# Five more seven-product quads in the SSM branch product, left factors fetched for each use, and side transfers moved to the queues of ScalarE and GpSimd

## The chip, the cores and the metric

The kernel runs on one core of one Trainium2 chip. Its engines are TensorE (PE, matrix products; PEld is its weight load), VectorE (DVE), ScalarE (ACT), GpSimd (POOL) and SyncE (SP, which here only issues transfers). SP, ACT and POOL can each start DMA transfers, each from a queue of its own that is worked off in order. The metric is the device time of one execution in microseconds.

## The reference

One layer of a hybrid block on 256 tokens of width 2048, all in float32:

```
proj = rms_norm(x, norm_w) @ w_in                 # 2048 x 18496 (q, k, v, z_a, z_s, xbc, dt, g_a, g_s)
o_a  = dilated_attention(q, k, v) * silu(z_a)     # 16 heads of 128, three patterns
xbc  = silu(causal_conv(xbc)); xs, B, C = split(xbc)
y    = rms_norm((ssd_scan(xs, dt, a, B, C) + d_skip * xs) * silu(z_s), ssm_norm_w)     # 256 x 4096
merged = sigmoid(g_a) * (o_a @ w_attn_branch) + sigmoid(g_s) * (y @ w_ssm_branch)
out  = rms_norm(x + merged @ w_out, final_norm_w)
```

The product that the change works on is `y @ w_ssm_branch`: 256 x 4096 by 4096 x 2048.

## The kernel before

**Precision.** Every operand is split in two float32r parts, high `h` (a copy by ScalarE, line 276) and low `l` (what is left, a subtraction by VectorE, line 277). A product is the sum of three matmuls: high by high, high by low, low by high.

**The stream of weights.** All weights lie in DRAM in units of 128 x 1024 (512 KB), in the order of use. A unit is loaded by SP into one of five ring buffers (tag `w`, line 265), split by ScalarE and VectorE into `h` and `l` (four buffers each), and used by TensorE. `FIRST[tag]` is the number of the first unit of a product. A step of another part can be hung behind a unit: `behind_unit(n, f)` runs `f` when unit `n` has been split.

**Order of stages.** First product and dt; then eight groups of the SSM (tags B, C, xs, zs; two units of weights for each 128 columns), each with convolution, decays and scan; then the product `ssm` in two column pairs, `("ssm", 0)` and `("ssm", 2)`; then `v`, the 16 heads (q, k, za), and `ga`, `attn`, `out`, each in two column pairs. The scheduler of the language puts the instructions of each engine in an order of its own, by priorities; the semaphores follow from the buffers.

**Pair products.** `gemm_pair` computes 256 rows by two blocks of 512 columns, step by step over quads: a quad is 256 of the inner dimension. `S_QUADS` says which quads are done by seven products instead of eight (a Strassen-like scheme), `Y_ORDERS` in which order the quads of `ssm` come.
- A plain quad: two units, each split by one ACTIVATE and one subtraction of 128 x 1024, and 2 x 2 x 2 x 3 = 24 matmuls of 128 x 512.
- A seven-product quad: 7 x 3 = 21 matmuls of 128 x 512. Its right factors: `wa` (512 KB), a presummed `wt` (512 KB) and `wc` (256 KB) are loaded; ScalarE and VectorE split `wa`, `wc` and `wt`, VectorE subtracts (line 557) and splits the rest. If the sums were not made before (`presum`), the raw unit is loaded as `wb` and VectorE makes the two sums in place (lines 549 and 555).
- Its left factors: four sums of quarters of the activations, made by `turn_x` on VectorE, split, and kept as a tile `sx`.

**Side work in the group stage.** `sum_jobs` makes presums ahead: `get` loads two tiles (512 and 256 KB) into a `place`, `add` makes two subtractions of 128 x 512 three units later (`SUM_LAG`), and `spill` writes the result to DRAM. There is one place for the SSM's 18 slots (three per group, `SUM_UNITS`); 22 jobs stand in the list, so the last four of `("v", 2)` are not made ahead. `keep_left` makes left factors and spills them; `fetch_left` loads them again. Six of the eight left factors of `ssm` go this way; those of quads 12 and 13 are made in place by `left_y`. A left factor that serves both pairs is loaded once and stays in SBUF with three of its four parts, the fourth in the activations themselves (`spare`).

**Queues and pacing.** All of these transfers, the fetches and the spills, are issued by SP, between the loads of the stream. So that they do not start too early, GpSimd first copies one column of the unit's `h` into the first column of the destination (lines 247, 251, 432, 638, 903): the transfer has to wait for that copy. Only `x` and the last norm's weights near the end are issued by ScalarE's queue.

Of the kernel before, what the change touches and what calls it, by code (L numbers as in the profile page):

```python
# [9 lines left out]
F32 = mybir.dt.float32  # L10
F32R = mybir.dt.float32r
AF = mybir.ActivationFunctionType
# [3 lines left out]
P = 128  # L16
# [180 lines left out]
def hybrid_block(ctx: ExitStack, tc: tile.TileContext, wall, xt, x, pk_d, cst_d, fw_d, out):  # L197
# [32 lines left out]
    ssm_pool = []  # L230

    def behind_unit(n, f):
        on_unit.setdefault(n, []).append(f)
# [4 lines left out]
    def spill(kept, key, name, src, shape):  # L238
        kept[key] = dram.tile([P, *shape], F32, name=name, tag=name)
        nc.sync.dma_start(kept[key], src)  # L240

    def sum_jobs(jobs, units, places):

        def get(tag, q, t, b11, behind):
            n = FIRST[tag] + 2 * q
            for dst, src in ((t, wall[n + 1]), (b11, wall[n, :, :512])):
                gp.tensor_copy(dst[:, 0:1], behind)
                nc.sync.dma_start(dst, src)

        def add(tag, q, t, b11, res, behind):  # L250
            gp.tensor_copy(res[:, 0:1], behind)
            ve.tensor_tensor(res[:, :512], t[:, :512], b11, ALU.subtract)
            ve.tensor_tensor(res[:, 512:], t[:, 512:], res[:, :512], ALU.subtract)
            spill(presum, (tag, q), f"t_{tag[0]}{tag[1]}_{q}", res, [UNIT])

        for n, ((tag, q), u) in enumerate(zip(jobs, units)):
            t, b11, res = places[n % len(places)]
            behind_unit(u, lambda behind, a=(tag, q, t, b11): get(*a, behind))
            behind_unit(u + SUM_LAG, lambda behind, a=(tag, q, t, b11, res): add(*a, behind))

# [6 lines left out]
    def unit(n, shape):  # L267
        if n not in loaded:
            load(n)
        w = loaded.pop(n)  # L270
        h = stream.tile([P, UNIT], F32R, name=f"h{n}", tag="h", bufs=H_BUFS)
        l = stream.tile([P, UNIT], F32R, name=f"l{n}", tag="l", bufs=H_BUFS)
        cuts = (0, UNIT // 2, UNIT) if n < N_FINE else (0, UNIT)
        with tc.high_priority(L_AHEAD) if n >= KT // UB else nullcontext():
            for a, b in zip(cuts, cuts[1:]):
                ac.activation(h[:, a:b], w[:, a:b], AF.Copy)  # L276
                ve.tensor_tensor(l[:, a:b], w[:, a:b], h[:, a:b].bitcast(F32), ALU.subtract)  # L277
# [407 lines left out]
    with tc.tile_pool(name="ssm", bufs=2) as sp:  # L685
# [205 lines left out]
        for c in GS_BEFORE[0]:  # L891
            gates(("gs", c), th_s, yT, hr_x)

        sums_at = big.tile([P, 4, UNIT], F32, name="sums_at", tag="yo1b")
        at = sums_at[:, 3]
        begin = FIRST[("xs", 4)]
        sum_jobs(
            SUMS_SSM, [FIRST[("B", g)] + n for g in range(1, 7) for n in SUM_UNITS],
            [(sums_at[:, 0], sums_at[:, 2, :512], sums_at[:, 1])],
        )  # L900

        def left_x(q, behind):
            gp.tensor_copy(at[:, 0:1], behind)
            keep_left(("x", q), two_kts(XT, q), 0, at)

# [71 lines left out]
    with tc.tile_pool(name="xp", bufs=1) as xp:  # L977
        sxs = {}
        ssm_room = room_of(xp.tile([P, ROOM_SSM * 512], F32, name="room_s", tag="room"), 0, ROOM_SSM)

        def left_y(q):
            spare = Y_SPARE[q]
            sx = new_sx(xp, sum(s == spare for s in Y_SPARE.values()), spare, f"y{q}")
            sxs[q] = turn_x(sx, ring(f"sxt_y{q}").rearrange("p (n m) -> p n m", n=2), two_kts(yT, q), spare)

        for q in SX_Y:
            if q in Y_LATE:
                continue
            fetch_left(sxs, xp, sum(s == Y_SPARE[q] for s in Y_SPARE.values()), ("y", q), two_kts(yT, q), Y_SPARE[q], plain_unit(("ssm", 0), Y_ORDERS[0].index(q) - 3 if q in S_QUADS[("ssm", 0)] else 12, Y_ORDERS[0]))
        for c in (0, 2):  # L990
            es, prods = gemm_pair(
                ("ssm", c), lambda kt: kt_of(yT, kt), 2 * KT, sxs, c == 2, {} if c else {2: [scale_gate], **{u: [lambda q=q: left_y(q)] for q, u in Y_LATE.items()}},
                1, Y_ORDERS[c], ssm_room,
# [19 lines left out]
    dist_c, count_c = dc[:, :384], dc[:, 384:]  # L1013
    behind_unit(FIRST[("v", 2)] + 1, lambda behind: fetch(dc, cst_d[:, :768], behind))
    room = room_of(big.tile([P, 6 * 512], F32, name="room_v", tag="yo0a"), 2, 2)
# [17 lines left out]
    with tc.tile_pool(name="att", bufs=2) as ap:  # L1033
# [33 lines left out]
        def mix(h, pT, za):  # L1067
# [10 lines left out]
            if h % 2 == 1 and q in ATT_QUADS:  # L1078
# [3 lines left out]
            SUMS_ATT, range(FIRST[("q", 0)] + 7, N_UNITS, ATT_EVERY),  # L1082
            [
                (th_a[:, i, :UNIT], th_a[:, 1, UNIT + 512 * i : UNIT + 512 * i + 512], th_a[:, 0, UNIT:])
                for i in range(2)
            ],
        )
# [28 lines left out]
    with tc.tile_pool(name="fin", bufs=2) as fp:  # L1116
# [36 lines left out]
        for n in range(4):  # L1153
            i, cs = n // 2, slice(n % 2 * UNIT, (n % 2 + 1) * UNIT)
            behind_unit(
                FIRST[X_BEHIND[n][0]] + X_BEHIND[n][1],
                lambda behind, i=i, cs=cs: fetch(fin[:, i, cs], x[i * P : (i + 1) * P, cs], behind, nc.scalar),
            )

        fw = big.tile([P, D], F32, name="fw", tag="yo0b")  # L1160
        for n, (tag, u) in enumerate(FW_BEHIND):
            cs = slice(n * UNIT, (n + 1) * UNIT)
            behind_unit(
                FIRST[tag] + u, lambda behind, cs=cs: fetch(fw[:, cs], fw_d[cs].partition_broadcast(P), behind, nc.scalar)
            )
# [106 lines left out]
```

## Time and profile before

| | |
|---|---|
| median of 3 runs | 1385.53 us (1385.44 to 1386.13) |
| profiled execution, first to last instruction (span) | 1383.8 us |
| TensorE busy | 1373.6 us, 99% of the span |
| VectorE busy | 1169.5 us, 85% |
| ScalarE busy | 835.5 us, 60% |
| GpSimd busy | 142.0 us, 10% |
| DMA | 345.00 MB, mean 249 GB/s |
| granted TensorE clock | 0.998 |

The profile shows one execution. Its own time is known as its span; what lies around the span (the launch and the end) is not in it, and the median of the runs shown is 1.7 us longer than the span. A busy TensorE is not TensorE at its best: matmuls overlap, so the time from the start of one to the start of the next is what counts, not the duration of one.

### The profile page before, as it was taken

To read this page: it belongs to the slowest core of one execution; us is meant where nothing else is said; L and a number is where in the kernel's file an instruction comes from. 1 tells how busy PE (TensorE), PEld (TensorE's weight loads), DVE (VectorE), ACT (ScalarE), POOL (GpSimd) and SP (SyncE) were. 2 spreads that over 40 slices of the span, in tenths; PEclk is the share of its full clock that TensorE was granted. 3 is DMA by queue.
4 is the path that set the end of the run, shared out by engine and by line. 5 is a ranking of instruction groups with operands and counts; after the bars stand their busy time and mean duration, and the time that the engine had idled before them with its cause. 6 is when DMAs were issued, how large, how long until landed. Compare 5 with 4: busy or idle time off the path is not lost.

```text
span 1383.8 us, 20696 instructions
## 1 busy us (share of the span) xinstructions
PE 1373.6 (99%) x7266; PEld 1169.9 (85%) x7266; DVE 1169.5 (85%) x1753; ACT 835.5 (60%) x1306; POOL 142.0 (10%) x226
## 2 busy tenths in 40 slices
PE   9999999999999999999999999999999999999997
PEld 8888888888888888888888888888888888888886
DVE  7898999987799898789889897777877788888897
ACT  7656677675667675766565554544544556655564
POOL 2301111101011100010001001111111000000112
PEclk9999999999999999999999999999999999999999
DMA  9767988868787866668677668888888757865773
GB/s 347 231 187 225 313 254 291 279 224 287 245 266 240 294 212 208 188 224 280 230 259 267 222 209 278 275 275 273 299 288 301 241 161 264 294 222 180 243 273 122
DMA packets 105080, 345.00 MB, mean 249 GB/s; under 512 B 11728, under 2 KB 13712, under 8 KB 104976
## 3 DMA queue, kind: packets, MB, share of 16 engines
q1 hardware_dynamic: 103536, 339.62, 74.0%
q10 hardware_dynamic: 1440, 4.06, 0.8%
q8 instruction: 57, 0.93, 0.3%
q14 instruction: 47, 0.39, 0.1%
HBM read 314.87 MB, written 28.77 MB: 248 GB/s over the span
## 4 chain that ended last, share of the span: by engine, by line
PE 97%; DMA 1%; DVE 1%; ACT 1%; issue 0%; SPq 0%; POOL 0%; POOLq 0%; DVEq 0%; ACTq 0%
PE ps_zs L329 8%; PE ps_xs L329 8%; PE ps_zs L332 4%; PE ps_q L329 4%; PE ps_za L329 4%; PE ps_k L329 4%; PE ps_xs L332 4%; PE ps_ssm L476 3%; PE ps_ssm L477 3%; PE ps_ssm L478 3%; PE ps_q L332 2%; PE ps_k L332 2%; PE ps_za L332 2%; PE ps_gs L414 2%; PE ps_gs L412 2%; PE ps_gs L413 2%
## 5 line engine op out<-in xcount | busy, mean ns | idle before, releaser
L276 ACT ACTIVATE h<-w 128x1024 fp32r<-128x1024 f32 (+1 forms) x398 | 413.9, 1047 | 318.0 <-issue 78.8
L277 DVE TENSOR_TENSOR l<-w,h 128x1024 fp32r<-128x1024 f32 (+1 forms) x398 | 479.4, 1211 | 124.2 <-ACT h L276 121.8
L329 PE MATMUL ps_zs<-XT,h 128*128 128x512 f32 x496 | 176.3, 397 | 0.0
L329 PE MATMUL ps_xs<-XT,h 128*128 128x512 f32 x496 | 175.9, 396 | 0.0
L332 PE MATMUL ps_zs<-XT,l 128*128 128x256 f32 x496 | 139.9, 282 | 0.0
L332 PE MATMUL ps_xs<-XT,l 128*128 128x256 f32 x496 | 139.8, 282 | 0.0
L329 PEld LDWEIGHTS ps_xs<-XT,h 128*128 128x128 f32 x496 | 93.3, 188 | 21.7
L329 PEld LDWEIGHTS ps_zs<-XT,h 128*128 128x128 f32 x496 | 93.4, 188 | 21.2
L332 PEld LDWEIGHTS ps_zs<-XT,l 128*128 128x128 f32 x496 | 93.7, 189 | 1.5 <-issue 0.7
L332 PEld LDWEIGHTS ps_xs<-XT,l 128*128 128x128 f32 x496 | 93.7, 189 | 0.4
L329 PE MATMUL ps_q<-XT,h 128*128 128x512 f32 x256 | 92.5, 405 | 0.2 <-ACT h L276 0.2
L329 PE MATMUL ps_k<-XT,h 128*128 128x512 f32 x256 | 89.9, 395 | 0.0
L329 PE MATMUL ps_za<-XT,h 128*128 128x512 f32 x256 | 89.7, 394 | 0.0
L543 ACT ACTIVATE ha<-wa 128x1024 fp32r<-128x1024 f32 x43 | 45.4, 1055 | 46.4 <-DMA wa<-in_wall 10.9
L332 PE MATMUL ps_q<-XT,l 128*128 128x256 f32 x256 | 71.2, 278 | 0.0
L332 PE MATMUL ps_k<-XT,l 128*128 128x256 f32 x256 | 71.1, 278 | 0.0
L332 PE MATMUL ps_za<-XT,l 128*128 128x256 f32 x256 | 71.1, 278 | 0.0
L544 DVE TENSOR_TENSOR la<-wa,ha 128x1024 fp32r<-128x1024 f32 x43 | 52.5, 1220 | 11.9 <-ACT ha L543 11.8
L782 ACT ACTIVATE gt<-acb,acT 128x128 f32<-128x128 f32 x128 | 44.2, 391 | 23.7 <-DMA acb<-acum_d 21.9
L329 PEld LDWEIGHTS ps_q<-XT,h 128*128 128x128 f32 x256 | 48.2, 188 | 11.5 <-ACT h L276 0.6
L329 PEld LDWEIGHTS ps_za<-XT,h 128*128 128x128 f32 x256 | 48.1, 188 | 11.3
L329 PEld LDWEIGHTS ps_k<-XT,h 128*128 128x128 f32 x256 | 48.1, 188 | 11.2
(688 smaller groups left out, 3325.1 us busy)
## 6 DMA issues: line engine op xcount, KB each, us to landing
w<-in_wall SPq DMA_DIRECT2D x394, 512.0 KB, 4.7
wa<-in_wall SPq DMA_DIRECT2D x43, 512.0 KB, 4.9
th_a<-in_wall SPq DMA_DIRECT2D x19, 512.0 KB, 5.6
sums_at<-in_wall SPq DMA_DIRECT2D x18, 512.0 KB, 4.7
acb<-acum_d SPq DMA_DIRECT2D x32, 256.0 KB, 4.0
t_ssm<-sums_at SPq DMA_DIRECT2D x13, 512.0 KB, 4.1
wt<-t_ssm SPq DMA_DIRECT2D x13, 512.0 KB, 5.4
th_a<-in_wall SPq DMA_DIRECT2D x19, 256.0 KB, 6.0
```

The costliest lines, as they stand in the source:

```text
L276: ac.activation(h[:, a:b], w[:, a:b], AF.Copy)
L277: ve.tensor_tensor(l[:, a:b], w[:, a:b], h[:, a:b].bitcast(F32), ALU.subtract)
L329: pe.matmul(acc, h[:, kk, :], m, start=(kt == 0), stop=False)
L332: pe.matmul(acc[:, S:], l[:, kk, :], m[:, :S], start=False, stop=(kt == KT - 1))
L412: pe.matmul(accs[i], xh, h[:, kk], start=(kt == 0), stop=False)
L413: pe.matmul(accs[i], xh, l[:, kk], start=False, stop=False)
L476: pe.matmul(acc, xh, h, start=start, stop=False)
L477: pe.matmul(acc, xh, l, start=False, stop=False)
L478: pe.matmul(acc, xl, h, start=False, stop=stop)
L543: ac.activation(h, src, AF.Copy)
L544: ve.tensor_tensor(l, src, h.bitcast(F32), ALU.subtract)
L782: ac.activation(g4[:, n, b], acb[:, j, b // 2 * P : b // 2 * P + P], AF.Relu, scale=-1.0, bias=sc[:, h : h + 1],)
```

## The change

1. The lists of quads: `("ssm", 0)` has nine seven-product quads (5 to 13), not seven; `("ssm", 2)` has eleven (2, 3, 5 to 13), not eight. The orders of the quads are new, with up to four seven-product quads in a row. The left factors of quads 12 and 13 are made earlier (behind quads 3 and 4 of the first pair).
2. The left factors of the other nine quads are made with all four parts, spilled, and fetched anew for each use, into a ring of five buffers (`Y_RING`), three quads ahead (`Y_AHEAD`): 16 fetches of 512 KB, not five of 384 KB and one of 512 KB.
3. Presums for the SSM and v: five slots per group, not three; 27 jobs, all of them made, not 18. Two places, not one; the result overwrites the loaded tile.
4. The side fetches (`side`) are issued by ScalarE's queue, in its program order behind the `h` copy of the unit on which they hang (`issue_after`: a place in the order, no semaphore). The spills are issued by GpSimd's queue. The pacing copies on GpSimd are gone; the subtractions of `add` and the left factors of x stand behind the unit's `l` in VectorE's order.

```diff
 S_QUADS = {
-    ("ssm", 0): (5, 7, 8, 10, 11, 12, 13), ("ssm", 2): (3, 5, 7, 8, 10, 11, 12, 13),
+    ("ssm", 0): (5, 6, 7, 8, 9, 10, 11, 12, 13), ("ssm", 2): (2, 3, 5, 6, 7, 8, 9, 10, 11, 12, 13),
...
-Y_ORDERS = {0: (0, 1, 2, 3, 5, 4, 7, 8, 6, 10, 11, 9, 12, 14, 13, 15), 2: (0, 3, 1, 5, 2, 7, 8, 4, 10, 11, 6, 12, 9, 13, 14, 15)}
-Y_LATE = {12: 4, 13: 6}
+Y_ORDERS = {0: (0, 1, 5, 2, 6, 7, 3, 8, 9, 4, 10, 11, 12, 14, 13, 15), 2: (0, 2, 1, 3, 5, 6, 4, 7, 8, 9, 14, 10, 11, 12, 13, 15)}
+Y_LATE = {12: 3, 13: 4}
+Y_AHEAD, Y_RING = 3, 5
-Y_SPARE = {q: int(q in S_QUADS[("ssm", 0)] and q in S_QUADS[("ssm", 2)]) for q in SX_Y}
+Y_SPARE = {q: int(q in Y_LATE) for q in SX_Y}
-SUM_UNITS = 2, 9, 16
+SUM_UNITS = 1, 5, 9, 13, 17
+    def side(dst, src, queue=nc.scalar):
+        with tc.issue_after(here["high"]):
+            queue.dma_start(dst, src)
     def spill(kept, key, name, src, shape):
         kept[key] = dram.tile([P, *shape], F32, name=name, tag=name)
-        nc.sync.dma_start(kept[key], src)
+        gp.dma_start(kept[key], src)
     def sum_jobs(jobs, units, places):
-        def get(tag, q, t, b11, behind):
+        def get(tag, q, t, b11):
             n = FIRST[tag] + 2 * q
-            for dst, src in ((t, wall[n + 1]), (b11, wall[n, :, :512])):
-                gp.tensor_copy(dst[:, 0:1], behind)
-                nc.sync.dma_start(dst, src)
-        def add(tag, q, t, b11, res, behind):
-            gp.tensor_copy(res[:, 0:1], behind)
-            ve.tensor_tensor(res[:, :512], t[:, :512], b11, ALU.subtract)
-            ve.tensor_tensor(res[:, 512:], t[:, 512:], res[:, :512], ALU.subtract)
-            spill(presum, (tag, q), f"t_{tag[0]}{tag[1]}_{q}", res, [UNIT])
+            side(t, wall[n + 1])
+            side(b11, wall[n, :, :512])
+        def add(tag, q, t, b11):
+            with tc.issue_after(here["low"]):
+                ve.tensor_tensor(t[:, :512], t[:, :512], b11, ALU.subtract)
+                ve.tensor_tensor(t[:, 512:], t[:, 512:], t[:, :512], ALU.subtract)
+            spill(presum, (tag, q), f"t_{tag[0]}{tag[1]}_{q}", t, [UNIT])
...
     def fetch_left(kept, pool, bufs, key, x, spare, u):
         def get(behind):
             sx = new_sx(pool, bufs, spare, f"{key[0]}{key[1]}")
-            gp.tensor_copy(sx[:, 0, 0, 0:1], behind)
-            nc.sync.dma_start(sx.bitcast(F32), lefts[key])
+            side(sx.bitcast(F32), lefts[key])
...
-        at = sums_at[:, 3]
+        at = sums_at[:, 2]
-            [(sums_at[:, 0], sums_at[:, 2, :512], sums_at[:, 1])],
+            [(sums_at[:, n], sums_at[:, 3, n * 512 : n * 512 + 512]) for n in range(2)],
...
+        for c in (0, 2):
+            for at, q in enumerate(Y_ORDERS[c]):
+                if q not in S_QUADS[("ssm", c)] or q in Y_LATE:
+                    continue
+                if at < Y_AHEAD and c == 2:
+                    u = plain_unit(("ssm", 0), 13, Y_ORDERS[0])
+                else:
+                    u = plain_unit(("ssm", c), max(at - Y_AHEAD, 0), Y_ORDERS[c])
+                fetch_left(sxs[c], xp, Y_RING, ("y", q), two_kts(yT, q), 0, u)
```

The fetches of `x`, of the last norm's weights and of the attention's constants, too, go by `side` without a pacing copy; the 19 presums of `ga`, `attn` and `out` keep their number and their units, with the result written over the loaded tile.

More of the change, by code (lines that the diff above doesn't have):

```diff
@@ L898, in hybrid_block @@
             SUMS_SSM, [FIRST[("B", g)] + n for g in range(1, 7) for n in SUM_UNITS],
-            [(sums_at[:, 0], sums_at[:, 2, :512], sums_at[:, 1])],
+            [(sums_at[:, n], sums_at[:, 3, n * 512 : n * 512 + 512]) for n in range(2)],
         )
         def left_x(q, behind):
-            gp.tensor_copy(at[:, 0:1], behind)
-            keep_left(("x", q), two_kts(XT, q), 0, at)
+            with tc.issue_after(here["low"]):
+                keep_left(("x", q), two_kts(XT, q), 0, at)
         for n, q in enumerate(SX_X + SX_V):
@@ L1013, in hybrid_block @@
     dist_c, count_c = dc[:, :384], dc[:, 384:]
-    behind_unit(FIRST[("v", 2)] + 1, lambda behind: fetch(dc, cst_d[:, :768], behind))
+    behind_unit(FIRST[("v", 2)] + 1, lambda behind: side(dc, cst_d[:, :768]))
     room = room_of(big.tile([P, 6 * 512], F32, name="room_v", tag="yo0a"), 2, 2)
@@ L1082, in hybrid_block @@
             SUMS_ATT, range(FIRST[("q", 0)] + 7, N_UNITS, ATT_EVERY),
[L1083 to L1086, printed above, removed]
+            [(th_a[:, i, :UNIT], th_a[:, i, UNIT : UNIT + 512]) for i in range(2)],
         )
@@ L1156, in hybrid_block @@
                 FIRST[X_BEHIND[n][0]] + X_BEHIND[n][1],
-                lambda behind, i=i, cs=cs: fetch(fin[:, i, cs], x[i * P : (i + 1) * P, cs], behind, nc.scalar),
+                lambda behind, i=i, cs=cs: side(fin[:, i, cs], x[i * P : (i + 1) * P, cs]),
             )
@@ L1163, in hybrid_block @@
             behind_unit(
-                FIRST[tag] + u, lambda behind, cs=cs: fetch(fw[:, cs], fw_d[cs].partition_broadcast(P), behind, nc.scalar)
+                FIRST[tag] + u, lambda behind, cs=cs: side(fw[:, cs], fw_d[cs].partition_broadcast(P))
             )
```

25 lines of the change are left out of this document (11 added, 14 removed).

## The prediction

> **What bounds the kernel now.** I read the page first: busy shares and the chain of work that ended last.
>
> ```profile
> PE 1373.6 (99%) x7266; PEld 1169.9 (85%) x7266; DVE 1169.5 (85%) x1753; ACT 835.5 (60%) x1306; POOL 142.0 (10%) x226
> ...
> PE 97%; DMA 1%; DVE 1%; ACT 1%; issue 0%; SPq 0%; POOL 0%; POOLq 0%; DVEq 0%; ACTq 0%
> ```
>
> TensorE carries 97% of the chain, VectorE is next by load. Busy alone would prove little, so the second view is that of the waits, for TensorE alone:
>
> ```profile
> PE warm L623 <- DVE ssq L620: 1.4, 1, 1.4
> PE ps_first L377 <- ACT h L276: 0.3, 1, 0.3
> PE ps_q L329 <- ACT h L276: 0.2, 1, 0.2
> ```
>
> Columns: total, times, longest. In the whole span TensorE waits for another engine three times, 1.9 us together, and none of it lies in a place where side transfers run. So neither the pacing copies nor SP's long queue costs anything today: a queue that runs better can win back at most 0.2 us (the wait of ps_q, behind v), and what counts is the number of matmuls. The third view, the pieces of the chain, gives the price of one in the `ssm` product (start, length, what):
>
> ```profile
> 654.19 0.91 PE ps_ssm L476 x4
> ```
>
> 0.91 us / 4 = 0.2275 us from start to start. A plain quad is 24 x 0.2275 = 5.46 us, a seven-product quad 21 x 0.2275 = 4.78 us. The product before has 15 seven-product quads and 17 plain ones: 723 matmuls, 164.5 us.
>
> **Fewer matmuls.** Nine and eleven seven-product quads instead of seven and eight: five quads lose three matmuls each, 15 x 0.2275 = 3.41 us off TensorE. Nothing on TensorE is added: left factors are made on VectorE and ScalarE, and the banks and the folds keep their number. This is the whole gain on offer, 0.25% of 1385.5 us, while 0.2% (2.8 us) is about what a measurement of this kernel can tell from no change. So 0.6 us of new waits on TensorE would make it "no change", and 6.2 us "slower". The rest of the work is to see whether the cover still holds.
>
> **VectorE in the ssm product.** The stages, by windows of my choice (length; then PE, PEld, DVE, ACT, POOL busy; clock; DMA share; GB/s); the second pair's first matmul is at about 667:
>
> ```profile
> 583.60:666.00 82.40, 82.40 (x369) 68.40 (x368) 70.66 (x86) 50.91 (x59) 4.79 (x7) 1.00 0.76 255
> 666.00:748.50 82.50, 82.50 (x365) 68.35 (x365) 73.26 (x77) 47.20 (x52) 2.28 (x3) 1.00 0.75 248
> ```
>
> and VectorE's instructions there in order of time (start, length):
>
> ```profile
> 673.85 2.35 DVE L277 TENSOR_TENSOR l<-w,h 128x1024 fp32r<-128x1024 f32 x2
> 676.12 1.22 DVE L544 TENSOR_TENSOR ltu<-wa,htu 128x1024 fp32r<-128x1024 f32 x1
> 677.25 1.22 DVE L544 TENSOR_TENSOR la<-wa,ha 128x1024 fp32r<-128x1024 f32 x1
> 678.39 0.69 DVE L544 TENSOR_TENSOR lc<-room_s,hc 128x512 fp32r<-128x512 f32 x1
> 678.99 1.22 DVE L544 TENSOR_TENSOR ltt<-wt,htt 128x1024 fp32r<-128x1024 f32 x1
> 680.12 1.22 DVE L557 TENSOR_TENSOR wa<-wa,wt 128x1024 f32<-128x1024 f32 x1
> ```
>
> From start to start a 128x1024 takes 1.13 us, a 128x512 0.60. A plain quad costs VectorE 2.27 us, a presummed seven-product quad 4 x 1.13 + 0.60 = 5.14, that is 0.36 us more than TensorE needs for it. Each conversion adds 2.87 us. First pair: 70.7 + 2 x 2.87 = 76.4 us against 82.4 - 2 x 0.68 = 81.0 (94%). Second pair: 73.3 + 3 x 2.87 = 81.9 against 82.5 - 3 x 0.68 = 80.5: 1.4 us too much. The lead pays for it. At the end of the second pair VectorE has already done this for v:
>
> ```profile
> 741.97 1.22 DVE L544 TENSOR_TENSOR ltt<-room_v,htt 128x1024 fp32r<-128x1024 f32 x1
> 743.10 2.52 DVE L277 TENSOR_TENSOR l<-w,h 128x1024 fp32r<-128x1024 f32 x2
> ```
>
> 3.7 us of work ahead, and v then needs less: its last four seven-product quads become presummed, which takes 4 x 2 x 0.60 = 4.8 us off VectorE there. Whether the order inside the second pair holds I add up by quads; what VectorE has done before TensorE starts on it, and what is left of the first pair's fold and gate, I take from today:
>
> ```profile
> 659.46 2.35 DVE L277 TENSOR_TENSOR l<-w,h 128x1024 fp32r<-128x1024 f32 x2
> ...
> 665.03 1.22 DVE L544 TENSOR_TENSOR ltt<-wt,htt 128x1024 fp32r<-128x1024 f32 x1
> ...
> 666.77 0.69 DVE L999 TENSOR_TENSOR tmp_ht<-ps_ssm,tmp_ht 128x512 f32<-128x512 f32 x1
> ...
> 671.51 1.28 DVE L1000 TENSOR_TENSOR th_s<-th_s,tmp_lt 128x512 f32<-128x512 f32 x2
> ```
>
> Done ahead: 3 x 1.13 = 3.4 us. Still to do: seven instructions of 128x512 (the third row to the last), 7 x 0.60 = 4.2. So VectorE ends a quad 0.8 us plus its own work up to there after the pair's start; TensorE wants the last part of a quad after all quads before it and 15 of its 21 matmuls (3.4 us). Quad 2, the first with seven products: 0.8 + 2.27 + 5.14 = 8.2 against 5.46 + 3.4 = 8.9. Quad 6, the end of the run 3, 5, 6: 0.8 + 2 x 2.27 + 4 x 5.14 = 25.9 against 2 x 5.46 + 3 x 4.78 + 3.4 = 28.7. Quad 13, the end of 10 to 13 (12 with its sums in place, 1.2 us more): 0.8 + 4 x 2.27 + 11 x 5.14 + 1.2 = 67.6 against 4 x 5.46 + 10 x 4.78 + 3.4 = 73.0. With VectorE at work all the time it holds, by less than 1 us at the start and by 3 to 5 later; I take 0, between a gain of 0.2 and a loss of 1.7 (rival one).
>
> **VectorE in the groups.** Five sum jobs per group, not three, in groups 1 to 5: 2 x 2 x 0.60 = 2.4 us more in each. Three more left factors (quads 2, 6 and 9): two 128x512 and four 128x128 instructions, 2 x 0.69 + 4 x 0.285 = 2.5 us each. The two fullest groups:
>
> ```profile
> 172.80:233.10 60.30, 60.30 (x367) 52.38 (x366) 56.45 (x94) 42.48 (x82) 8.91 (x19) 1.00 0.85 274
> 233.10:293.70 60.60, 60.60 (x364) 52.31 (x364) 56.30 (x96) 41.99 (x80) 6.59 (x16) 1.00 0.83 275
> ```
>
> 56.5 + 2.4 = 58.9 of 60.3, and 56.3 + 2.4 + 2.5 = 61.2 of 60.6: 0.6 us of work slides into the gate product that follows. The sums and left factors are due hundreds of us later; the splits go first by priority. I take 0, bounds 0 and 1.
>
> **ScalarE and the queues.** GpSimd's pacing and SP's issues, as they are for the SSM's sums (min/median/max in ns), and the landing of side transfers:
>
> ```profile
> L247 POOL COPY sums_at<-h x36: 178/457/1617, 113.7 to 477.2; 128x1 f32<-128x1 f32 x36
> L248 SPq DMA_DIRECT2D sums_at<-in_wall x36: 327/358/659, 113.9 to 477.6; - x36
> L251 POOL COPY sums_at<-h x18: 183/1182/1652, 119.1 to 484.4; 128x1 f32<-128x1 f32 x18
> L252 DVE TENSOR_TENSOR sums_at<-sums_at x18: 681/692/694, 120.4 to 485.7; 128x512 f32<-128x512 f32 x18
> ...
> L450 DVE TENSOR_TENSOR sums_at<-sums_at x11: 279/285/289, 132.3 to 519.1; 128x128 f32<-128x128 f32 x11
> ...
> DMA to landing us min/median/max: 3.1/4.9/7.1
> ```
>
> and one issue on ScalarE's queue, from the fetches of `x` near the end:
>
> ```profile
> L639 ACTq DMA_DIRECT2D fin<-in_x x4: 335/352/353, 1287.1 to 1335.4; - x4
> ```
>
> ScalarE takes over 54 + 38 issues of sum jobs, 25 of left factors and one of constants: 118 x 0.35 = 41 us, besides its 835.5 busy. In a group that is 10 x 0.35 = 3.5 on top of 42.5 of 60; in the second pair nine fetches (3.2 us) and three conversions (ScalarE has four splits instead of two, some 1.7 us each) on 47.2: 55.5 of 80. It stays below VectorE, so 0. SP loses as many issues and the waits for GpSimd, and the stream cannot be later for it: no gain, since TensorE does not wait. GpSimd loses the copies and gets 64 spills. A transfer issued by GpSimd is not in this trace; the nearest rows are an issue of SP (0.33 us) and a GpSimd copy that had to wait (1.6 us). Even 1.6 + 7.1 us to landing is less than the five units (about 13.6 us, at 8 x 0.34 us for a unit) between `add` and the next use of the place. Cover: those five units; if it went, ScalarE's next `get` would be late. I take 0; bounds 0 and rival three.
>
> A rule speaks against this move. The Trainium skill ("SBUF — State Buffer", section "SBUF: two separate sides") says that descriptors of a transfer from the GpSimd queue are generated on GpSimd, which VectorE's two-port instructions lock out, so that such a transfer can sit until VectorE is done. The copies of up to 1617 ns agree with a GpSimd that waits beside VectorE; a transfer of its own no row shows. By the rule the sum would be the same unless the delay passes those five units.
>
> **DMA.** The fetches of left factors grow from 2.5 MB to 16 x 0.524 = 8.4, the five conversions add 0.26 MB each: 41.5 MB (255 and 248 GB/s above) become 48.7 in 161.5 us, 302 GB/s. In a run of seven-product quads it is 1.31 + 0.52 = 1.83 MB in 4.78 us, 384 GB/s. What the core can do shows in this window:
>
> ```profile
> 460.00:465.00 5.00, 5.00 (x31) 4.34 (x30) 4.89 (x8) 3.61 (x6) 1.02 (x2) 1.00 1.03 419
> ```
>
> 419 GB/s. So a run is just carried, with the ring's lead in front. I take 0; late tiles would show first as waits of ScalarE, of which some are there today (the waits of the two pairs alone):
>
> ```profile
> ACT ha L543 <- DMA wa<-in_wall: 10.9, 3, 4.9
> ACT h L276 <- PE ps_ssm L478: 10.2, 8, 2.2
> DVE la L544 <- ACT ha L543: 8.2, 5, 3.1
> ```
>
> 4.9 us of lateness at once is absorbed by four buffers of `h` and `l` today; the second row shows ScalarE waiting for TensorE to free one, that is, being far ahead.
>
> **Sum.** -3.41 + 0 + 0 + 0 = -3.4 us. The execution profiled would have a span of 1380.4; the median stands 1.7 us above the span, so 1382.1.
>
> **Rivals.** One: VectorE becomes the bound in the second pair. For it: 81.9 us of work in 80.5, and VectorE idles for ScalarE (the 8.2 us before `la` are of the two pairs). With 1.4 too much, 4 of such idle time and 3.7 of lead, TensorE waits 1.7 us: 1383.8, up to 1386 if the groups add theirs. Against: idle time shrinks where an engine has a backlog. Two, the slower side: ScalarE's queue stops. A fetch into the ring of five waits on ScalarE until TensorE has read the tile of five uses before; 11 of the 16 fetches reuse a tile, and all splits stand behind. For it: three fetches hang on one plain quad in the second pair (6, 7, 8, then 9, 10, 11), close to the use they have to outwait. Against: the order lets a fetch stand later. It decides for "slower" from 6.2 / 11 = 0.56 us of TensorE per fetch; at 0.7 us it is 7.7: 1389.8. Three: spills by GpSimd land after the five units, `get` stops ScalarE in the groups; 27 jobs at 0.2 us are 5.4: 1387.5, at 0.35 us 1391.6. Four: late tiles eat exactly the gain, nothing is won: 1385.5.
>
> **Chances and range.** Forecast 0.54 (its own range 1381.5 to 1382.7), rival one 0.25, two 0.15, three 0.04, four 0.02. Faster: the forecast, 0.54. Slower: two and most of three, 0.18. Within 0.2%: the rest, 0.28. The range runs from 1381.4 (the wait of ps_q and a little more gone) to 1388.3, where "slower" begins; it leaves out rival two and the worse half of three.
>
> **What would show it.** Right: 708 matmuls of 128x512 in the ssm product, its length 161 us at 0.2275 a piece; TensorE's waits still below 2 us; v's `wb` gone. Wrong: waits of PE for `l`, `ltt` or `ltu` between 650 and 760 (one); for `h` after an ACTq fetch of `sx_y`, with ScalarE idle for PE or DMA before it (two); the same for `sums_at` in 110 to 500 (three). I would be most wrong if ScalarE's order puts the fetches too early.

## The result and the profile after

The changed kernel is slower: 1405.16 us median of four runs (1397.18 to 1413.7) against 1385.49 us of the kernel before on the same chip, ratio 1.0142 [1.0118, 1.0165]. The forecast was 1382.1 us. The profiled execution is the quickest of the four, 1397.18 us with a span of 1395.4 us, 11.6 us more than before; what is said from the trace explains these 11.6 us. The other runs are longer by up to 16.5 us.

The page after, busy shares and the chain that ended last:

```profile
PE 1372.8 (98%) x7251; PEld 1164.5 (83%) x7251; DVE 1189.1 (85%) x1791; ACT 845.1 (61%) x1314; POOL 65.9 (5%) x152
...
PE 74%; DMA 10%; issue 6%; DVE 4%; ACT 4%; ACTq 0%; SPq 0%; POOL 0%; POOLq 0%; DVEq 0%
```

TensorE's 15 matmuls fewer are there (7266 to 7251), yet its share of the chain falls from 97% to 74%: DMA, VectorE and ScalarE now carry 18% of the path, and 6% is issue, time in which the engine waited for nothing that the profile shows. The busy share hides that, 98% against 99%. What TensorE waits for in the whole span (total, times, longest):

```profile
PE pp_ssm L481 <- ACT ha L548: 2.5, 1, 2.5
PE ps_ssm L481 <- ACT h L282: 1.7, 3, 1.0
PE ps_xs L335 <- ACT h L282: 1.5, 1, 1.5
PE warm L628 <- DVE ssq L625: 1.4, 1, 1.4
PE pp_ssm L481 <- ACT htu L548: 1.4, 2, 1.2
PE ps_xs L338 <- DVE l L283: 1.3, 1, 1.3
PE ps_ssm L481 <- DMA sx_y<-sxd_y: 1.0, 1, 1.0
PE ps_zs L335 <- ACT h L282: 1.0, 1, 1.0
PE ps_first L383 <- ACT h L282: 0.9, 1, 0.9
PE pp_ga L481 <- ACT htu L548: 0.8, 1, 0.8
```

Three waits have become a dozen small ones, in three places: the groups (`ps_xs`, `ps_zs`), the product `ssm`, and `ga`. Nearly all are for a split of a weight tile by ScalarE or VectorE; one, 1.0 us, is for a fetched left factor (`sx_y`). The windows (length; PE, PEld, DVE, ACT, POOL busy; clock; DMA share; GB/s), two of groups, then the two pairs of `ssm`:

```profile
173.00:236.20 63.20, 60.88 (x366) 52.27 (x365) 57.25 (x96) 42.28 (x80) 3.81 (x12) 1.00 0.90 316
236.20:296.60 60.40, 60.35 (x366) 52.30 (x365) 57.28 (x98) 41.67 (x80) 4.76 (x13) 1.00 0.90 320
587.60:670.00 82.40, 80.84 (x362) 66.38 (x359) 73.73 (x88) 49.19 (x60) 0.14 (x1) 1.00 0.79 272
670.00:757.00 87.00, 81.56 (x350) 64.72 (x349) 76.82 (x79) 54.77 (x59) 0.59 (x1) 1.00 0.80 278
```

The product is not shorter by 3.4 us but longer: in its second pair TensorE idles 5.4 us of 87. VectorE idles 10.2 us of the same 87, so its total load is not the bound. In the groups the DMA's share went from 0.85 and 0.83 to 0.90, and the rate from 274 and 275 to 316 and 320 GB/s.

For each kernel below I add up the gaps between the starts of TensorE's weight matmuls beyond the usual spacing (over 0.15 us), by stage, in the one profiled execution; the columns are medians, ratios, and these extra microseconds. The columns also hold what a halved clock adds, up to 1.7 us for each stretch of 3.4 us (last section). Such stretches lie in e2 (two in the groups, three in the product), e3 (groups), e5 (groups and product), e6 (product, one of 6.8 us), e8 (`v` and `ga`), e9 (`ga`), e10 and e11 (product) and e12 (two in the groups, five in the product); the others have none before their end. Single executions differ besides: without the clock's part the product has 8.0 to 9.1 us of extra time in after, e3, e10, e11 and e16, which all leave it alone.

| kernel | median us | ratio [95%] | groups | ssm | v | ga |
|---|---|---|---|---|---|---|
| before | 1385.49 | 1 | 0 | 0 | 0 | 0.2 |
| after | 1405.16 | 1.0142 [1.0118, 1.0165] | 4.8 | 8.5 | 0 | 1.8 |
| e1 queues alone | 1389.59 | 1.0033 [1.0020, 1.0047] | 0.2 | 0 | 0 | 1.6 |
| e2 quads alone | 1418.32 | 1.0232 [1.0214, 1.0249] | 11.2 | 20.3 | 0 | 0.2 |
| e3 spills by SP | 1399.30 | 1.0106 [1.0087, 1.0124] | 5.0 | 8.0 | 0 | 0.2 |
| e4 old quads | 1391.26 | 1.0041 [1.0026, 1.0056] | 3.5 | 0 | 0 | 2.7 |
| e5 no left fetch | 1402.92 | 1.0132 [1.0115, 1.0149] | 8.1 | 9.1 | 0 | 2.1 |
| e6 own room for wt | 1401.68 | 1.0120 [1.0105, 1.0135] | 6.7 | 8.3 | 2.3 | 2.0 |
| e7 less VectorE | 1395.95 | 1.0077 [1.0062, 1.0092] | 5.9 | 2.9 | 0.3 | 2.2 |
| e8 three slots | 1406.98 | 1.0152 [1.0136, 1.0167] | 0.3 | 5.9 | 10.4 | 3.8 |
| e9 third pair of buffers | 1398.74 | 1.0089 [1.0069, 1.0109] | 6.2 | 4.8 | 0 | 4.2 |
| e10 sums not added | 1398.85 | 1.0103 [1.0078, 1.0127] | 0.9 | 10.8 | 0 | 1.9 |
| e11 sums not fetched | 1393.64 | 1.0058 [1.0043, 1.0073] | 0 | 9.7 | 0 | 2.0 |
| e12 GpSimd subtracts | 1430.65 | 1.0319 [1.0304, 1.0335] | 13.6 | 28.2 | 0.4 | 0.2 |
| e13 all three causes away | 1381.75 | 0.9974 [0.9963, 0.9985] | 0 | 1.7 | 0 | 0.2 |
| e14 ScalarE's queue only | 1386.28 | 1.0005 [0.9996, 1.0015] | 0.9 | 0 | 0 | 0.2 |
| e15 old quads, spills by SP | 1387.18 | 1.0010 [1.0000, 1.0020] | 1.8 | 0 | 0 | 0.2 |
| e16 two causes away | 1393.00 | 1.0055 [1.0040, 1.0070] | 1.4 | 8.5 | 0 | 0.2 |

After: 4.8 + 8.5 + 1.6 more waits - 3.4 for the matmuls = 11.5, of the 11.6 us by which its span is longer.

### The profile page after: what moved, and what is told of

It reads as the page before. It is cut to its first block, busy times and chain, and to the rows that moved or that the text cites. A ratio compares the mean times of both kernels' runs of the same rounds, so it can differ in the third digit from the quotient of the medians.

```text
span 1395.4 us, 20578 instructions
## 1 busy us (share of the span) xinstructions
PE 1372.8 (98%) x7251; PEld 1164.5 (83%) x7251; DVE 1189.1 (85%) x1791; ACT 845.1 (61%) x1314; POOL 65.9 (5%) x152
## 3 DMA queue, kind: packets, MB, share of 16 engines
q10 hardware_dynamic: 18432, 53.75, 11.5%
## 4 chain that ended last, share of the span: by engine, by line
PE 74%; DMA 10%; issue 6%; DVE 4%; ACT 4%; ACTq 0%; SPq 0%; POOL 0%; POOLq 0%; DVEq 0%
PE ps_zs L335 6%; PE ps_xs L335 5%; DMA acb<-acum_d 4%; PE ps_k L335 3%; PE ps_q L335 3%; PE ps_za L335 3%; PE ps_zs L338 3%; PE ps_xs L338 3%; PE ps_gs L420 2%; PE ps_gs L418 2%; PE ps_gs L419 2%; DMA w<-in_wall 2%; PE ps_out L481 2%; PE ps_out L482 2%; PE ps_out L483 2%
## 5 line engine op out<-in xcount | busy, mean ns | idle before, releaser
L282 ACT ACTIVATE h<-w 128x1024 fp32r<-128x1024 f32 (+1 forms) x388 | 403.6, 1047 | 307.3 <-issue 60.7
L283 DVE TENSOR_TENSOR l<-w,h 128x1024 fp32r<-128x1024 f32 (+1 forms) x388 | 468.3, 1212 | 127.6 <-ACT h L282 126.2
L548 ACT ACTIVATE ha<-wa 128x1024 fp32r<-128x1024 f32 x48 | 50.7, 1057 | 46.5 <-PE ps_v L483 12.0
L549 DVE TENSOR_TENSOR la<-wa,ha 128x1024 fp32r<-128x1024 f32 x48 | 58.7, 1223 | 12.1 <-ACT ha L548 11.6
L549 DVE TENSOR_TENSOR ltu<-wa,htu 128x1024 fp32r<-128x1024 f32 x43 | 52.6, 1222 | 12.8 <-ACT htu L548 12.7
L548 ACT ACTIVATE htu<-wa 128x1024 fp32r<-128x1024 f32 x43 | 45.2, 1052 | 24.9 <-PE ps_ssm L483 6.2
```

The source lines that it names most:

```text
L282: here["high"] = ac.activation(h[:, a:b], w[:, a:b], AF.Copy).ins
L283: here["low"] = ve.tensor_tensor(l[:, a:b], w[:, a:b], h[:, a:b].bitcast(F32), ALU.subtract).ins
L548: ac.activation(h, src, AF.Copy)
L549: ve.tensor_tensor(l, src, h.bitcast(F32), ALU.subtract)
```

## The experiments

**Which part of the change costs.** e1 keeps the quads, left factors, slots and the one place of before and takes only the new queues (the sums are written over the loaded tile, as after); e2 takes the quads, the fetched left factors and five slots, but the old queues with a pacing copy before each fetch.

```diff
 e1, against after
-SUM_UNITS = 1, 5, 9, 13, 17
+SUM_UNITS = 2, 9, 16
 (S_QUADS, Y_ORDERS, Y_LATE, Y_SPARE, the loading of left factors and the single place: as before)
 e2, against after
-    def side(dst, src, queue=nc.scalar):
-        with tc.issue_after(here["high"]):
-            queue.dma_start(dst, src)
+    def side(dst, src, behind, queue=nc.sync, first=None):
+        gp.tensor_copy(dst[:, 0:1] if first is None else first, behind)
+        queue.dma_start(dst, src)
...
-        gp.dma_start(kept[key], src)
+        nc.sync.dma_start(kept[key], src)
```

> The kernel before (seven and eight seven-product quads, left factors of ssm kept in SBUF, three sum slots per group, one place) with only the queues changed: side fetches by ScalarE, spills by GpSimd, no pacing copies. Theory Q (the queues: side transfers run beside the stream instead of in line with it, so stream tiles land later and TensorE waits): most of the loss of 20 us shows here, 1395 to 1405 us. Theory W (the work: more bytes and more VectorE work in the groups and in the ssm product): no loss here, 1384 to 1387 us.

> The changed kernel with all its quads, fetched left factors and five sum slots, but with the queues of before: side fetches and spills by SP, each fetch paced by a GpSimd copy. Theory Q: the gain of fewer matmuls appears, 1381 to 1385 us. Theory W: the loss stays, 1395 to 1410 us.

The queues alone cost 0.33%, the quads on the old queues 2.3%: more than the whole change. So the new queues do not cause most of the loss; they save the dense version 13 us (1418.3 to 1405.2), and my second rival, that ScalarE's queue stops on the ring, falls: the loss is there without that queue, and e5 below keeps it with 11 of the 16 fetches left out.

e3 is the changed kernel with SP's spills; e4 is the changed kernel with the quads and orders of before, and so with five sum jobs and three left factors fewer in the groups.

```diff
 e3
-        gp.dma_start(kept[key], src)
+        nc.sync.dma_start(kept[key], src)
 e4: S_QUADS[("ssm", 0)], S_QUADS[("ssm", 2)], Y_ORDERS and Y_LATE of before
```

> The changed kernel with only the spills back on SP's queue. If the spills from GpSimd do the harm (theory G, a part of Q): 1382 to 1387 us. If ScalarE's fetches or the work do it: within 5 us of the changed kernel, 1397 to 1410.

> The changed kernel with the quad lists, orders and late left factors of before (seven and eight), everything else as changed: new queues, fetched left factors, five sum slots. The product has 15 matmuls more (+3.4 us). Theory W with the dense quads as the cause: the waits in the ssm product go, 1389 to 1393 us, with the groups' 4 us left. Theory Q: 1397 us or more.

With the old quads the product has no extra time, so its 8.5 us belong to the dense quads and their order. With SP's spills `ga`'s extra time is gone. The place of that is the spill of a left factor of `o`, whose tile sits in a buffer that the splits also use. The tile's view, after, and then e3 (who waited: total, times):

```profile
L247 POOL DMA_DIRECT2D sxd_o<-sxt_o x4: 531/532/533, 995.5 to 1141.3; - x4
...
  ACT htu L548: 5.3, 1
...
DMA to landing us min/median/max: 4.5/5.5/6.4
```

```profile
L247 SPq DMA_DIRECT2D sxd_o<-sxt_o x4: 327/327/327, 994.2 to 1140.3; - x4
...
  ACT htu L548: 3.0, 1
...
DMA to landing us min/median/max: 4.3/4.5/4.7
```

Issued by GpSimd the spill takes 1 us longer to land in the median and 1.7 at worst, `htu` waits 5.3 us instead of 3.0, and TensorE 1.6 us more.

**Why the dense quads cost.** Four kernels change something about them. e5 leaves out 11 of the 16 fetches of left factors. e6 leaves out 13 (three tiles are fetched and stay) and gives `wt` two buffers of its own. e7 leaves out the subtraction of line 562 in `ssm`. e9 leaves out 13 fetches, too, and uses the room for a third pair of `ht` and `lt` buffers.

```diff
 e5
+            if key[0] == "y" and len(stay) >= Y_RING:
+                stay.append(stay[len(stay) - Y_RING])
+                kept[key[1]] = left_parts(stay[-1], x, spare)
+                return
...
+            if key[0] == "y":
+                stay.append(sx)
 e6, besides e5
-Y_AHEAD, Y_RING = 3, 5
+Y_AHEAD, Y_RING = 3, 3
-        ssm_room = room_of(xp.tile([P, ROOM_SSM * 512], ...), 0, ROOM_SSM)
+        ssm_room = room_of(xp.tile([P, (4 + ROOM_SSM) * 512], ...), 2, ROOM_SSM)
 e7
-                ve.tensor_tensor(two(wa), two(wa), t2, ALU.subtract)
+                if tag[0] != "ssm":
+                    ve.tensor_tensor(two(wa), two(wa), t2, ALU.subtract)
 e9, besides e5
-Y_AHEAD, Y_RING = 3, 5
+Y_AHEAD, Y_RING = 3, 3
+        tl_s = xp.tile([P, 2, UNIT], F32R, name="tl_s", tag="tl_s")
+        ssm_room["tl"] = [(tl_s[:, 0], tl_s[:, 1])]
```

> The changed kernel without 11 of the 16 fetches of left factors in the ssm product: the first five tiles are fetched, the later quads use them again (their factors are those of another quad). Quads, matmuls, VectorE's and ScalarE's work stay. Theory D (data: the fetches of 0.52 MB per quad beside the stream make the right factors late, ScalarE waits, TensorE waits): the waits in the ssm product go, 1388 to 1394 us. Theory V (VectorE, 5.14 us per quad against TensorE's 4.78) and theory R (the ring of five holds two tiles per seven-product quad and turns over too slowly): no gain beyond 2 us of the changed kernel, 1399 to 1408.

> As e5_no_left_fetch, with three left tiles that stay, and the room of the other two given to two buffers for wt, so that a seven-product quad of ssm holds one tile of the ring instead of two. Theory R: waits in the ssm product go here and not in e5, 1388 to 1394. Theory D: same as e5 within 2 us. Theory V: 1399 to 1408, as the changed kernel.

> The changed kernel without the subtraction wa - wt (line 562) in the ssm product: VectorE has 1.13 us less per seven-product quad, 20 x 1.13 = 22.7 us in all; ring tiles come free that much earlier, too. Transfers and matmuls stay. Theory V: the waits in the ssm product go, 1388 to 1394. Theory D: a gain of 0 to 5 us, 1399 to 1406. Theory R lies between, since a ring tile is held 1.1 us shorter of some 12: 1396 to 1403.

> As e5_no_left_fetch (three left tiles that stay, no further fetches), with a third pair of buffers for the splits of wt and of wa - wt in the ssm product (two pairs before). Theory M: with two pairs ScalarE can split wa - wt of the next quad only when TensorE is through with the present one, so a run of seven-product quads has no lead; the waits in the ssm product go, its length falls from about 172 us (e5) to 163, the time from 1402.9 to 1392 to 1396. Theory V (VectorE's work as such): same as e5 within 2 us.

The fetches are not it: 9.1 us stay, 7.5 without the clock's part. One 128x1024 subtraction less per seven-product quad, 1.13 of its 5.14 us on VectorE, takes 5.6 of the 8.5 us away; a third pair of split buffers takes away 4.3 of e5's 9.1, of which 1.6 is the clock's. Each falls short of what I expected of a sole cause: e7's 1396 us lie between the ranges set for VectorE and for the ring of loaded tiles, which its edit frees earlier, too; e9's 1398.7 are above 1392 to 1396. So the cost hangs on VectorE's time per quad and on how far the splits can run ahead. Whether more buffers for loaded tiles help as well stays open. e6's time is that of e5, but most of its 8.3 us is one late load at the start of the product and the clock behind it (TensorE's row, then a window):

```profile
605.94 1.19 PE L488 MATMUL pp_ssm<-htt,sx_y 128*128 128x512 f32 x2 [3.11 <-DMA room_s<-in_wall]
```

```profile
605.70:612.50 6.80, 6.44 (x14) 4.63 (x15) 6.80 (x10) 5.50 (x7) 0.00 (x0) 0.50 0.87 292
```

3.1 us of waiting and 3.4 of half clock leave 1.8 for the rest of that product, while its `v` loses 2.3. Open, too, is what part the new order (up to four dense quads in a row) has: no run varies it alone.

The longest wait of after shows how VectorE's time and the buffers are tied; its timelines, ScalarE, SP, VectorE and TensorE (start, length, what, in brackets the idle time before and what ended it):

```profile
717.28 1.06 ACT L548 ACTIVATE htu<-wa 128x1024 fp32r<-128x1024 f32 x1 [1.21 <-PE ps_ssm L483]
...
722.60 1.04 ACT L282 ACTIVATE h<-w 128x1024 fp32r<-128x1024 f32 x1
726.40 1.06 ACT L548 ACTIVATE ha<-wa 128x1024 fp32r<-128x1024 f32 x1 [2.75 <-DMA wa<-in_wall]
```

```profile
715.27 2.60 SPq L271 DMA_DIRECT2D w<-in_wall  x2
719.81 0.33 SPq L527 DMA_DIRECT2D wa<-in_wall  x1
```

```profile
718.56 1.22 DVE L549 TENSOR_TENSOR ltu<-wa,htu 128x1024 fp32r<-128x1024 f32 x1
```

```profile
724.66 0.39 PE L483 MATMUL pp_ssm<-htt,sx_y 128*128 128x512 f32 x1
727.50 0.50 PE L481 MATMUL pp_ssm<-ha,yT 128*128 128x512 f32 x1 [2.46 <-ACT ha L548]
```

At 717.28 ScalarE could split `wa` only when TensorE had let go of an `ht` buffer. VectorE's last read of that `wa` starts at 718.56 and ends at 719.78; 0.03 us later SP, which stood waiting, issues the next `wa` into the room. It is ready at 726.40, 6.6 us after its issue, and TensorE, which had run dry at about 725, goes on at 727.5. I read it as a loop: TensorE frees a split buffer, ScalarE splits, VectorE subtracts and frees a loaded tile, SP loads, ScalarE splits. Before this wait VectorE had stood idle four times between 695 and 708 us, around the plain quad 4, 6.0 us together; one of the four, with what ScalarE waited for:

```profile
703.27 1.06 ACT L548 ACTIVATE htu<-wa 128x1024 fp32r<-128x1024 f32 x1 [2.64 <-PE ps_ssm L483]
```

```profile
704.36 1.22 DVE L549 TENSOR_TENSOR ltu<-wa,htu 128x1024 fp32r<-128x1024 f32 x1 [2.10 <-ACT htu L548]
```

From 708 to 727 us VectorE then works without a break, and TensorE runs dry all the same. In the two pairs ScalarE's waits for TensorE stand ahead of those for most tiles:

```profile
ACT htt L548 <- PE pp_ssm L483: 10.2, 7, 2.4
ACT h L282 <- DMA w<-in_wall: 8.3, 5, 4.9
ACT ha L548 <- PE ps_ssm L483: 6.7, 4, 2.9
ACT htu L548 <- PE ps_ssm L483: 6.2, 4, 2.6
```

Such waits are in the kernel before, too; there the largest sum was for `h` (10.2 us), with 5.1 for `htt`. A dense quad fills both pairs of `ht` and `lt`, so being "ahead" is capped at about one quad; and a load of `wa`, 5.6 us in the median of the two pairs, is longer than a quad of 4.78 us.

**Why the groups cost.** e8 goes back to three slots; e10 leaves out the subtractions of the sum jobs of `ssm` and `v`, e11 25 of their 27 pairs of fetches; e12 moves these subtractions and those of line 562 in `ssm` to GpSimd, with SP's spills.

```diff
 e8
-SUM_UNITS = 1, 5, 9, 13, 17
+SUM_UNITS = 2, 9, 16
 e10, in add
-            with tc.issue_after(here["low"]):
...
+            if tag[0] not in ("ssm", "v"):
+                with tc.issue_after(here["low"]):
+                    ve.tensor_tensor(t[:, :512], t[:, :512], b11, ALU.subtract)
+                    ve.tensor_tensor(t[:, 512:], t[:, 512:], t[:, :512], ALU.subtract)
 e11, in get
+            if tag[0] in ("ssm", "v") and len(got) >= 2:
+                return
+            got.append(q)
 e12
-            with tc.issue_after(here["low"]):
-                ve.tensor_tensor(t[:, :512], t[:, :512], b11, ALU.subtract)
...
+            eng = gp if tag[0] in ("ssm", "v") else ve
+            eng.tensor_tensor(t[:, :512], t[:, :512], b11, ALU.subtract)
...
-                ve.tensor_tensor(two(wa), two(wa), t2, ALU.subtract)
+                (gp if tag[0] == "ssm" else ve).tensor_tensor(two(wa), two(wa), t2, ALU.subtract)
```

> The changed kernel with three sum slots per group instead of five: 18 presums, the last nine seven-product quads of v sum in place. The groups carry 9 x 0.79 MB less of fetches and 0.52 MB less of spills each, and 2.4 us less of VectorE. If the five slots make the groups' waits (4 us in the profile): 1399 to 1402; if v then gets late: 1403 to 1408. The ssm product should show the same waits as in the changed kernel.

> The changed kernel without the two subtractions of the sum jobs of ssm and v (the raw tile is spilled): VectorE has 27 x 1.2 us less in the groups; transfers stay. If VectorE's load makes the groups' loss (theory V): the groups lose 0 to 1 us against the kernel before, not 4 to 8, and the whole is 4 to 7 us below the changed kernel. If the transfers do (theory D): the groups still lose 4 us or more.

> The changed kernel without 25 of the 27 pairs of fetches of the sum jobs of ssm and v: 0.79 MB each less beside the stream in the groups and 50 issues of ScalarE less; subtractions and spills stay. Theory D: the groups lose 0 to 1 us against the kernel before; theory V: still 4 us or more.

> The changed kernel with spills by SP (as e3_spill_sp, 1399.3) and the subtractions of the sum jobs and of wa - wt in the ssm product on GpSimd instead of VectorE: the same result, VectorE relieved of 55 us. If VectorE is the limit and GpSimd works beside it: the gain of the 15 matmuls comes out, 1381 to 1386 us. If GpSimd takes above 4 us for a 128x1024, or holds VectorE up while it reads: 1395 or more.

Three slots clear the groups (0.3 us) and only shift the cost: `v`, whose nine presums are then missing, loses 10.4. Leaving out either half of a sum job clears the groups, too. The first of the two windows of groups, in e10 and then in e11:

```profile
173.00:236.00 63.00, 63.00 (x381) 54.66 (x380) 54.26 (x90) 44.56 (x88) 4.79 (x15) 1.00 0.91 314
```

```profile
173.00:236.00 63.00, 63.00 (x382) 54.85 (x381) 58.83 (x101) 44.15 (x88) 4.34 (x13) 1.00 0.76 250
```

With the DMA as full as after (0.91) but 54.3 us of VectorE, TensorE does not stop here; nor does it with 58.8 us of VectorE but a DMA at 0.76. It takes both, the sums' transfers and their subtractions, which is why the load added to either, taken alone, looked free. (e11 takes 50 issues off ScalarE as well; they are not needed for the loss, since in e2, where SP makes them, the groups lose 11.2 us.) What is late at the two longest stops of TensorE in the groups of after is a stream tile, and `acb`, 256 KB for the scan, behind which the next split stands in ScalarE's order:

```profile
202.09 1.06 ACT L282 ACTIVATE h<-w 128x1024 fp32r<-128x1024 f32 x1 [1.50 <-DMA w<-in_wall]
```

```profile
455.07 0.69 ACT L787 ACTIVATE gt<-acb,acT 128x128 f32<-128x128 f32 x2 [2.85 <-DMA acb<-acum_d]
```

How the subtractions make such a late load reach TensorE is not shown: at the second of these stops VectorE itself idles 2.2 us.

e12 shows that GpSimd is no way out. Its groups of instructions (busy, mean ns):

```profile
L258 POOL TENSOR_TENSOR sums_at<-sums_at 128x512 f32<-128x512 f32 x27 | 54.1, 2002 | 203.4 <-DMA sums_at<-in_wall 186.3 <-DVE zs L403 10.8 <-PE xtp L806 6.3
L562 POOL TENSOR_TENSOR wa<-wa,wt 128x1024 f32<-128x1024 f32 x18 | 52.5, 2919 | 158.9 <-DVE la L549 108.3 <-DMA wt<-t_ssm 35.0 <-DVE var_y L600 15.6
```

2.92 us instead of VectorE's 1.22, inside the loop above: the product loses 28 us, some 8 of them by the halved clock.

**Whether that is all.** e13 takes the three causes away at once and keeps the 15 matmuls fewer (edits of e3, e7, e9 and e11 together, so with 13 of the 16 fetches left out, not 11). e16 takes away only e3's and e11's. e14 is e1 with SP's spills, e15 is e4 with SP's spills.

```diff
 e13 = e3 + e7 + e9 + e11;  e16 = e3 + e11;  e14 = e1 + e3;  e15 = e4 + e3
```

> The changed kernel with all three suspected costs taken away at once: spills by SyncE's queue; 25 of the 27 pairs of fetches of the sum jobs of ssm and v left out; the subtraction wa - wt of the ssm quads left out, with a third pair of ht and lt buffers and 11 of the 16 fetches of left factors left out to make room for it. The 15 matmuls fewer stay. If the three causes (the groups' late sums, the dense quads of the product, the spill in ga) are the whole loss, the gain of 15 x 0.2275 = 3.4 us must now appear: 1381.5 to 1383.5, TensorE's extra time below 1 us in each stage. If something else in the change costs too: 1385 or more with extra time that none of the three stages' waits explains.

> The changed kernel with two costs taken away: spills by SyncE's queue, and 25 of the 27 pairs of fetches of the sum jobs of ssm and v left out. The dense quads of the product stay as they are. If the product then still loses its 8 to 10 us for 3.4 us gained: 1389.5 to 1393. If the product's loss came from what the groups leave undone (VectorE late into it) or from transfers on the same queues: below 1387.

> Quads, resident left factors, sum slots and places of before; side transfers by ScalarE's queue without pacing copies, but the spills by SyncE's queue and not GpSimd's. The new queues with GpSimd's spills gave 1389.6. If the spills that land late hold ga and are the loss of the queues: 1385 to 1386.3 (nothing left of it, ga's extra time 0.2 us). If ScalarE's issues cost by themselves (the rival of ScalarE's queue in a mild form): 1387.5 or more, with extra time in the groups or the product.

> The changed kernel (left factors fetched for each use, five sum slots, side transfers on ScalarE's queue) with the 7 and 8 quads of before and the spills by SyncE's queue. The same with GpSimd's spills gave 1391.3, of it 3.5 us of extra time in the groups and 2.7 in ga. If these are two causes that add: 1388 to 1389.5, the groups' 3.5 us still there and ga's gone. If the groups' part also comes from GpSimd's queue (spills run there too): below 1387.

e13 takes 1381.75 us: without the three costs the gain is there. That it lies within 0.4 us of the forecast is luck in part. Of the 4.2 us by which its span is shorter than before, the product gives 1.6 and the groups, where e13 leaves work out, 1.2 (from first matmul to first matmul of the next stage); the rest is spread in small pieces. TensorE's waits in it:

```profile
PE ps_ssm L492 <- ACT hc L559: 1.5, 1, 1.5
PE warm L640 <- DVE ssq L637: 1.4, 1, 1.4
PE ps_first L388 <- ACT h L287: 0.2, 1, 0.2
```

Its product shows 1.7 us of extra time, against the 1 us that I had set as the limit. e16 says that the product's loss does not come from what the groups leave undone: with the groups nearly clear it is 8.5 us as before. e14 is no different from the kernel before (1.0005 [0.9996, 1.0015]): ScalarE's queue itself costs nothing that can be measured, and what the queues cost in e1 is GpSimd's spills. e15 is quicker than I expected (1387.2, not 1388 or more): the groups show 1.8 us there, not 3.5. So GpSimd's spills cost more than `ga` shows; by the ratios of after and e3, e4 and e15, e1 and e14 they cost 0.36, 0.31 and 0.28%, that is 5.0, 4.3 and 3.9 us, of which the traces show 1.6, 2.5 and 1.4 in `ga`. (The intervals of after and e3 overlap, those of the other two pairs do not.) Where the rest is stays open; the groups do not settle it, with 4.8 and 5.0, 3.5 and 1.8, 0.2 and 0.9 us in the three pairs.

No kernel that does the whole work beats the one before.

## Why the prediction was wrong, step by step

- **"Fewer matmuls"** held. The gain is real and of the size forecast: the step had -3.4, and in e13 the product's start-to-start length shrinks by 1.6 us beside its 1.7 us of extra time, together 3.3.
- **"VectorE in the ssm product"** failed; it was put at 0 with a bound of 1.7; the product lost 8.5. The sentence that failed is "With VectorE at work all the time it holds, by less than 1 us at the start and by 3 to 5 later". The sum of the durations was nearly right as a limit and wrong as a schedule: VectorE cannot work all the time, since the lead of 3 to 5 us that the sum lives on is cut short by the buffers: by the two pairs of `ht` and `lt`, as e9 shows, and perhaps by the five loaded tiles. Around a plain quad it stands still, in the next run of dense quads it is late, and a late subtraction also delays a load. VectorE idles 10.2 us of 87 while TensorE waits 5.4.
- **"VectorE in the groups"** failed: 0, bounds 0 and 1, measured 4.8. The 2.4 us per group are there; what was missing is that they and some 42 to 45 GB/s more meet in the same stage. e10 and e11 show that either alone is carried.
- **"DMA"** took 0 on the ground that 419 GB/s had been seen. The wrong question: the rate was held, the latency was not. From 113 to 583 us a stream tile lands after 5.2 us in the median, where it was 4.8, and `acb` after 4.5, where it was 4.0. The side tiles show it most, with 6.3 us in the median and 10.8 at most, where it was 4.9 and 7.1:

```profile
L237 ACTq DMA_DIRECT2D sums_at<-in_wall x54: 334/335/564, 113.4 to 448.2; - x54
...
DMA to landing us min/median/max: 3.1/6.3/10.8
```

- **"ScalarE and the queues"** was right on ScalarE (e14) and wrong on the spills: their cover, the five units until the next `get`, belongs to the sums; the left factors of `o` go the same way and hold a split buffer in `ga`. The price is 0.28 to 0.36%. The rule of the Trainium skill ("SBUF — State Buffer", section "SBUF: two separate sides") that a transfer from GpSimd's queue can sit while VectorE runs two-port instructions spoke against this move. It agrees in sign with the issue of 532 ns instead of 327 and the landing of 5.5 us instead of 4.5; a lockout as such no run here shows.
- **The rivals.** One named the right engine and place (the second pair) and asked too little, 1.7 us, as it still priced a shortage of work time and not a loop. Its sign, waits of PE for `l`, `ltt` or `ltu`, hardly came: in the product PE waited 5.6 us for ScalarE's `ha`, `h` and `htu`, which stand further round the loop, and 0.4 us for `ltt`. Two fell; of its kind there is one wait of 1.0 us for `sx_y`. Three had a real mechanism: ScalarE does wait for spills in the groups (15.5 us in e1, the longest 5.6; 6.6 in e14, where SP issues them), but TensorE loses nothing by it there (0.2 us in e1), and what it loses it loses in `ga`, which the rival did not price. Four, late loads, was there as a part of the groups' loss, which with the other losses was more than the gain. My 0.18 for "slower" stood mostly on rival two, for a reason that was not the cause.

The median lies 8 us above the profiled execution. Its runs had granted clocks of 0.999, 0.993, 0.997 and 0.994, in the order 1397.18, 1413.7, 1404.1, 1406.23 us; 0.006 of 1412 us is 8.5 of the 16.5 us between the first two. The other half I take to be longer waits in those runs; they were not profiled.

## What to carry to other kernels

Where an engine needs more time than the bound engine in some steps and less in others, the sum over the stage says nothing until the buffers between them can hold the lead: count it in buffers, and go once round the loop from the freed buffer to the next load, its latency included. Two additions that each fit (work on a nearly full engine, traffic on a nearly full DMA) have to be tried together: here each alone was carried, and both were not. A gain of 3.4 us was here less than what each of two side effects cost (8.5 and 4.8 us), on an engine, VectorE, that already stood at 89 to 94% in those stages.

## What the hardware showed beyond this

**A long stall is paid twice.** After a pause TensorE's granted clock falls to half for a few us. The windows of e3 around its 3.9 us wait in the groups, then of e2 around one of 4.7 us in the product:

```profile
450.00:456.00 6.00, 2.18 (x13) 1.66 (x12) 2.39 (x3) 2.80 (x8) 0.00 (x0) 1.00 0.60 194
456.00:461.00 5.00, 4.94 (x19) 4.29 (x20) 4.96 (x7) 3.71 (x8) 0.00 (x0) 0.66 0.95 249
```

```profile
664.00:671.00 7.00, 2.25 (x10) 1.60 (x9) 0.76 (x2) 1.46 (x2) 0.43 (x1) 0.96 0.81 284
671.00:675.00 4.00, 4.00 (x13) 3.11 (x13) 4.00 (x5) 2.96 (x4) 0.00 (x0) 0.64 0.50 167
```

In e3 the clock is 0.66 in the 5 us after the pause: at half speed for 0.34 x 5 / 0.5 = 3.4 us, which costs up to 1.7 us. The Trainium skill ("TensorE: Matmul & The Clock Gate", section "What's actually happening") has a gate that works in windows of about 3.4 us and halves the clock after an idle one; the length of the dip agrees. A pause as long as a window is not needed here: in e2 the clock is 0.50 from 469.1 to 472.5 us, behind a pause of 1.9 us, and in e5 from 461.2 to 464.6, behind one of 1.8, while the 2.5 us of after have no dip behind them. So a pause of about 2 us can halve the clock and need not. The profiled execution of after has no dip but the one at the very end, which the kernel before has, too, and it is the quickest. A kernel with waits of this size scatters (1397 to 1414 us), while the one before, run beside it, stays within 1.3 us; that the dips make the scatter is my reading, since the slower runs were not profiled.
